# Squares added by VectorE, three last products by Pool, and gate blocks placed between a part's gates and its down products

## The chip, the cores and the metric

One core of one Trainium2 chip runs the kernel. The metric is the device time of one execution in microseconds (us), the median of several runs. The engines are named as the profile names them: PE (TensorE, with PEld for its weight loads), DVE (VectorE), ACT (ScalarE), POOL (GpSimd), and SP, whose queue issues all the DMAs here. Each engine executes its instructions in the order in which the program lists them; when the first waits, all behind it wait too.

## The reference, cut to what matters

The input x has 512 tokens of 1024 features. A block of four stages (a SwiGLU feed-forward, a mixer with a convolution and a recurrent scan, a second feed-forward, a norm) is followed by two layers, an "even" one (Fourier mixing and attention) and an "odd" one (a gated linear recurrence), and a last norm. The parts that this change touches:

```python
def rms_norm(x, g):
    xf = x.astype(jnp.float32)
    y = xf * lax.rsqrt(jnp.mean(xf * xf, axis=-1, keepdims=True) + RMS_EPS)
    return (y * g.astype(jnp.float32)).astype(x.dtype)

def swiglu(x, w_gate, w_up, w_down):      # 1024 -> 2816 -> 1024
    return (jax.nn.silu(x @ w_gate) * (x @ w_up)) @ w_down
...
    x = x + 0.5 * swiglu(rms_norm(x, ffn1_norm[l]), ...)
    x = x + token_mixer(rms_norm(x, mix_norm[l]), ...)
    x = x + 0.5 * swiglu(rms_norm(x, ffn2_norm[l]), ...)
    return rms_norm(x, final_norm)
```

The even layer begins with a second norm right behind `final_norm`, so two sums of squares of the same x are needed there: `s1` of x, and `s2` of x times the gain of `final_norm`.

## The kernel before

Features lie on the partitions: x is eight tiles `x[0]` to `x[7]` of 128 features by 512 tokens. Every product in float32 precision is made of three matmuls (`mm3`): each operand is split into a high part (`xh`, `h`, `wh`) and a low part (`xl`, `l`, `wl`), and high by high, low by high and high by low are added in one PSUM tile (`pm`). A `gemm` over 1024 features is thus 24 matmuls of 128x512.

A weight group (128x1024, 512 KB) takes this way: a DMA into `raw` (3 buffers), a cast to `wh` by ACT or DVE (4 buffers), a subtraction on DVE to `wl` (4 buffers). While the feed-forwards run, `put_low` also prepares the weights of later stages: it loads a group, splits it and stores its low part in DRAM (the DMA `low<-wl`), two groups for each of the gates 0 to 19 and one for each down product of the first two parts. The stage that needs them loads `raw` and `wl<-low`.

`rms` splits the scaled x, and `sumsq` squares the tiles on ACT and adds them up in `acc`, tile by tile, on Pool; `fold` splits `acc` into `h` and `l` and sums it over the partitions by two matmuls against ones (`rones`). In `ffn` 22 gates of 128 hidden features each are worked in three parts (8, 8 and 6). Gate `gi` is 24 matmuls for `pg`, 24 for `pu`; then DVE multiplies both by `rstd`, ACT takes the Silu, Pool multiplies the two, and ACT and DVE split the result into `h` and `l`. After the gates of a part come its eight down products (`ffn_d`), each a gemm over the part's `h` and `l`: three matmuls for each gate, the youngest gate's last. `last_norm` does the final norm in two halves of 256 tokens (`hf` 0 and 1); its last step multiplies the eight tiles by gain and by the reciprocal root (a PSUM tile) on DVE, and each product is stored by a DMA `y<-x`.

Nothing is issued as it is written. The kernel records its operations, and a list scheduler (`Rec.schedule`) simulates the engines offline with the costs of `_cost` and takes, on each engine, the ready operation of the lowest priority (its place in the written order plus a `bias`, for instance `late` for the sums of squares). The order found is then the order on the chip. All instructions therefore carry line L555 (`emit`).

Of the kernel before, what the change touches and what calls it, by code (L numbers as in the profile page):

```python
# [8 lines left out]
F32 = mybir.dt.float32  # L9
F32R = mybir.dt.float32r  # L10
AF = mybir.ActivationFunctionType
ALU = mybir.AluOpType
# [18 lines left out]
KT = 8  # L31
# [566 lines left out]
def _cost(o, outs, ins):  # L598

    n = _elems(outs[0]) if outs else 1  # L600
    psum = any("PSUM" in str(a.space) for a in ins)
    o.port = not any("PSUM" in str(a.space) for a in ins + outs) and n > 32 and o.fn not in ("tensor_reduce", "reciprocal")
    if o.eng == "tensor":
        if o.fn == "matmul":
            m = _elems(ins[0])
            k = int(ins[0].shape[0])
            up = lambda i: 32 if i <= 32 else 64 if i <= 64 else 128
            o.mode = up(k), up(m)
            one = "float32r" in str(ins[0].dtype)
            c = n / 2.4 + 13.5 if one else max(n, m) / 0.6 + 10.0  # L610
            o.load = n / (2.4 if one else 0.6) * o.mode[0] * o.mode[1] / 16384.0
            if not one and m <= 64 and k <= 64:
                c = 31.0 if n <= 64 else 105.0
        else:
            o.mode = 128, 128
            c = 109.0
            o.load = 50.0
        return c, 0.0
    if o.fn == "dma_start":
        run = min(_run(a) for a in outs + ins)  # L620
        return 480.0, _elems(outs[0]) * 4 * int(outs[0].shape[0]) / (360.0 if run >= 512 else 150.0)
    if o.eng == "scalar":
        c = 0.833 * n + (52.0 if psum else 94.0) + (185.0 if "accum_out" in o.kw else 0.0)
        return c + (93.0 if any(hasattr(o.kw.get(k), "tensor") for k in ("scale", "bias")) else 0.0), 0.0
    if o.eng == "gpsimd":
        k = {"memset": 0.76, "tensor_scalar": 1.2}.get(o.fn, 1.95)
        return k * n + 73.0, 0.0
    c = 69.0 if n > 16 else 105.0
    if o.fn == "tensor_tensor" and any(len(a.ap) > 1 and abs(list(a.ap)[-1][0]) >= 16 and list(a.ap)[-1][1] > 1 for a in ins):
        c += 0.9 * n  # L630
    if o.fn in ("tensor_scalar", "scalar_tensor_tensor"):
        c += 59.0 * sum(1 for a in ins[1:] if _elems(a) == 1 and n > 1)
    if o.fn == "reciprocal":
        return 6.25 * n + c, 0.0
    if o.fn == "tensor_tensor_scan":
        return 2.08 * n + c, 0.0
    if o.fn == "tensor_reduce":
        return 1.04 * _elems(ins[0]) + c, 0.0
    if o.fn in ("tensor_copy", "tensor_scalar", "memset") and not psum:
        return 0.52 * n + c, 0.0  # L640
    return 1.04 * n + c, 0.0
# [6 lines left out]
class Net:  # L648
    def __init__(self, tc, a, ctx, wbufs=(3, 4, 4), slots=76):
        self.tc, self.a = tc, a  # L650
        self.nc = self.rec = Rec(tc.nc)
        self.cp = ctx.enter_context(tc.tile_pool(name="cst", bufs=1))
        self.wp = ctx.enter_context(tc.tile_pool(name="wgt", bufs=1))
        self.wbufs = dict(zip(("raw", "wh", "wl"), wbufs))
        self.tp = ctx.enter_context(tc.tile_pool(name="act", bufs=1))
        self.sp = ctx.enter_context(tc.tile_pool(name="small", bufs=4))
        self.pm = ctx.enter_context(tc.tile_pool(name="pmm", bufs=8, space=PSUM))
        self.dp = ctx.enter_context(tc.tile_pool(name="dram", bufs=1, space=bass.MemoryType.DRAM))
        self.n = 0
        self.slots = slots  # L660
        self.late = 60
        self.low, self.later, self.behind, self.far = {}, [], 40, None
        nc = self.nc
        self.cst = self.cp.tile([128, _NC], F32, name="cst")
        self.vec = self.cp.tile([128, _NV], F32, name="vec")
        nc.sync.dma_start(out=self.vec, in_=a["vec"])
        self.load_x(a["xT"])
        nc.sync.dma_start(out=self.cst, in_=a["cst"])
        self.ident = self.c("ident")
        self.cr = {}  # L670
        for m in ("ones", "bones"):
            self.cr[m] = self.cp.tile([128, 128], F32R, name="r" + m)
            nc.vector.tensor_copy(self.cr[m], self.c(m))
        self.eps6 = self.cst[:, _COFF["eps"]:_COFF["eps"] + 1]
        self.epsg = self.cst[:, _COFF["eps"] + 1:_COFF["eps"] + 2]
        self.one = self.cst[:, _COFF["eps"] + 3:_COFF["eps"] + 4]
# [127 lines left out]
        self.nc.vector.scalar_tensor_tensor(l, src, g, h.bitcast(F32), op0=ALU.mult, op1=ALU.subtract)  # L804
        return h, l

    def sumsq(self, gains=None):

        nc = self.nc
        acc = self.T(p="acc")  # L810
        for k in range(KT):
            if k == 0:
                q = acc
            else:
                q = self.T(p="sq")
            if gains is None:
                nc.scalar.activation(q, self.x[k], AF.Square)
            else:
                nc.scalar.activation(q, self.x[k], AF.Square, scale=gains(k))
            if k:  # L820
                nc.gpsimd.tensor_tensor(acc, acc, q, ALU.add)
        ps = self.P()
        self.fold(ps, "ones", acc)
        return ps
# [16 lines left out]
        nc.vector.tensor_scalar(r, r, -0.5 * scale, 1.5, op0=ALU.mult, op1=ALU.add)  # L841
        nc.vector.tensor_tensor(out, out, r, ALU.mult)

    def rms(self, gname):

        xs = [self.split_scaled(self.x[k], self.v(gname, k)) for k in range(KT)]
        self.rec.bias = self.late
        ps = self.sumsq()
        rstd = self.T(p="rstd")
        self.rsqrt(rstd, ps, 1.0 / D, 1e-6)  # L850
        self.rec.bias = 0
        return xs, rstd


    def ffn(self, n):
        nc = self.nc
        xs, rstd = self.rms(n + "_norm")
        g0 = 0
        for ch, nk in enumerate((8, 8, 6)):
            hs = []  # L860
            for gi in range(g0, g0 + nk):
                wg = self.group(n + "_g", gi)
                pg = self.P()
                self.gemm(pg, wg, xs)
                wu = self.group(n + "_u", gi)
                pu = self.P()
                self.gemm(pu, wu, xs)
                t = self.T()
                nc.vector.tensor_tensor(t, pg, rstd, ALU.mult)
                nc.scalar.activation(t, t, AF.Silu)  # L870
                u = self.T()
                nc.vector.tensor_tensor(u, pu, rstd, ALU.mult)
                nc.gpsimd.tensor_tensor(u, u, t, ALU.mult)
                hs.append(self.split(u))
                if gi < 20:
                    self.put_low(2)
            g0 += nk
            for m in range(8):
                wd = self.group(f"{n}_d{ch}", m)
                ps = self.P()  # L880
                self.gemm(ps, wd, hs)
                xm = self.x[m]
                nc.vector.scalar_tensor_tensor(xm, ps, 0.5, xm, op0=ALU.mult, op1=ALU.add)
                if ch < 2:
                    self.put_low(1)


    def mixer(self):
# [457 lines left out]
    def _even(self):  # L1346
        nc = self.nc
        V, G, A, PE = nc.vector, nc.gpsimd, nc.scalar, nc.tensor
        x = self.x
# [1 line left out]
        o1, o2 = _VOFF["final_norm"], _VOFF["even_norm_2"]  # L1351
        V.tensor_tensor(g12, self.vec[:, o1:o1 + 8], self.vec[:, o2:o2 + 8], ALU.mult)
        xs = [self.split_scaled(x[k], g12[:, k:k + 1]) for k in range(KT)]
        s1 = self.sumsq()
        rstd1 = self.T(p="rs1")
        self.rsqrt(rstd1, s1, 1.0 / D, 1e-6)
        s2 = self.sumsq(lambda k: self.v("final_norm", k))
# [379 lines left out]
    def last_norm(self, hf):  # L1737
# [4 lines left out]
        s0 = slice(256 * hf, 256 * hf + 256)  # L1742
        if hf == 0:

            w = self.sm(1, tag="fw", bufs=1)
            o = A.activation(w, self.one, AF.Sqrt)
            o.deps.append(next(p for p in reversed(self.rec.ops[:-1]) if p.table))
        acc, q7 = (self.T(shape=(128, 512), p="sq")[:, 0:256] for _ in range(2))
        for k in range(KT):
            q = acc if k == 0 else q7 if k == KT - 1 else self.T(p="sq")[:, 0:256]  # L1750
            A.activation(q, x[k][:, s0], AF.Square)
            if 0 < k < KT - 1:
                G.tensor_tensor(acc, acc, q, ALU.add)
        on = self.c("ones")
        m = self.sm(2, tag="fn", bufs=8)
        for q, first in ((acc, True), (q7, False)):
# [16 lines left out]
        for t in range(2):  # L1773
            PE.matmul(ps[:, t * 128:t * 128 + 128], r[:, t:t + 1].to_broadcast([128, 128]), self.ident,
                      start=True, stop=True)
        for k in range(KT):
            V.scalar_tensor_tensor(x[k][:, s0], x[k][:, s0], self.v("final_norm_2", k), ps, op0=ALU.mult, op1=ALU.mult)
            nc.sync.dma_start(out=self.a["y"][:, k, s0], in_=x[k][:, s0])

    def all(self):  # L1780
# [2 lines left out]
        mix = [("w_in", t) for t in (5, 9, 1, 6, 10, 2, 7, 11, 3, 13, 17, 21, 14, 18, 22, 15, 19, 23, *range(26, 42))]  # L1783
        mix += [("w_out_a", h) for h in range(4)] + [("w_out_b", h) for h in range(4)] + [("w_o", g) for g in range(8)]
        n = len(self.rec.ops)
        self.later = mix
        self.ffn("ffn1")

        w = [o for o in self.rec.ops[n:] if o.fn == "dma_start"][:2]
        l = [o for o in self.rec.ops[:n] if o.fn == "dma_start"]  # L1790
# [31 lines left out]
```

## Time and profile before

| | |
|---|---|
| time, median of 3 runs | 1879.77 us (1878.92 to 1880.1) |
| the profiled execution's own time | 1883.26 us |
| its span from first to last instruction | 1881.5 us |
| mean granted clock of PE | 0.993 |
| busy share of PE, DVE, ACT, POOL | 98%, 68%, 45%, 13% |

The span leaves 1.76 us of the execution's time outside. A granted clock of 1.00 is full speed (2.4 GHz) and 0.5 half speed (1.2 GHz); a window in which part of the time was at half speed shows a number between.

### The profile page before, as it was taken

The page shows a single profiled execution, that of the slowest core. Times are in us where ns is not written, and L with a number is a line of the kernel's source. Part 1 is how long each engine was busy: PE and PEld are TensorE (multiplying, and loading weights), DVE is VectorE, ACT ScalarE, POOL GpSimd, SP SyncE. Part 2 cuts the span into 40 slices and gives each one's busy share as a digit, 9 for nine tenths or more (in the row PEclk, how much of TensorE's full clock was granted, in tenths as well). Part 3 has the DMA queues.
Part 4 walks back from the last instruction along what each step waited for, and adds up shares of the span by engine and source line. Part 5 has one row for each costly group of instructions (what it writes and reads, how often), then busy time and mean ns, then how long its engine had stood idle before and what let it go on. Part 6 is the DMA issues. An engine that isn't in the chain of part 4 may idle for free.

```text
span 1881.5 us, 26365 instructions
## 1 busy us (share of the span) xinstructions
PE 1842.7 (98%) x10324; PEld 1540.2 (82%) x10324; DVE 1272.1 (68%) x1956; ACT 852.2 (45%) x1180; POOL 246.4 (13%) x193
## 2 busy tenths in 40 slices
PE   7999999999999999999998999999999999999998
PEld 6878878887788887888887887888999888888887
DVE  7766665579857434477467567965478965899773
ACT  5333433365324333444344335422255554998771
POOL 2101100113203002211010017010000010000001
PEclk9999999999999999999999999999999999999999
DMA  7788896445533444578788773322221125556552
GB/s 249 271 302 282 293 299 201 121 152 162 179 121 112 152 137 160 197 260 308 251 281 288 252 261 107 115 66 69 90 68 59 65 79 191 178 191 211 191 179 102
DMA packets 120398, 341.10 MB, mean 181 GB/s; under 512 B 33872, under 2 KB 36176, under 8 KB 120272
## 3 DMA queue, kind: packets, MB, share of 16 engines
q1 hardware_dynamic: 120272, 339.41, 54.0%
q8 instruction: 81, 1.33, 0.3%
q14 instruction: 45, 0.37, 0.1%
HBM read 277.76 MB, written 61.60 MB: 180 GB/s over the span
## 4 chain that ended last, share of the span: by engine, by line
PE 73%; DMA 11%; DVE 11%; ACT 3%; issue 2%; POOL 0%; SPq 0%; DVEq 0%; ACTq 0%; POOLq 0%
PE pm L555 69%; DVE wl L555 5%; PE pw L555 4%; DMA low<-wl 2%; DMA raw<-o_in 2%; ACT wh L555 2%; DVE t L555 2%; DMA raw<-ffn_d 1%; DMA raw<-ffn_u 1%; DVE l L555 1%; DMA raw<-gw 1%; DMA raw<-w_in 1%; DMA raw<-w_out_a 1%; DVE wh L555 0%; DVE u L555 0%
## 5 line engine op out<-in xcount | busy, mean ns | idle before, releaser
L555 ACT CAST wh<-raw 128x1024 fp32r<-128x1024 f32 (+1 forms) x334 | 347.1, 1041 | 687.6 <-PE pm L555 278.4
L555 PE MATMUL pm<-xh,wh 128*128 128x512 f32 x1488 | 583.1, 392 | 8.4 <-ACT xh L555 8.2
L555 PE MATMUL pm<-xl,wh 128*128 128x512 f32 x1488 | 582.0, 391 | 2.5 <-DVE xl L555 2.5
L555 PE MATMUL pm<-xh,wl 128*128 128x512 f32 x1488 | 582.3, 391 | 1.1 <-DVE wl L555 1.0
L555 DVE TENSOR_TENSOR wl<-raw,wh 128x1024 fp32r<-128x1024 f32 (+1 forms) x302 | 386.3, 1282 | 202.2 <-DMA low<-wl 92.0
L555 PEld LDWEIGHTS pm<-xh,wh 128*128 128x128 f32 x1488 | 280.3, 188 | 67.2 <-ACT xh L555 9.4
L555 PEld LDWEIGHTS pm<-xl,wh 128*128 128x128 f32 x1488 | 280.4, 188 | 62.5 <-DVE xl L555 5.2
L555 PEld LDWEIGHTS pm<-xh,wl 128*128 128x128 f32 x1488 | 280.2, 188 | 60.5 <-DVE wl L555 2.8
L555 PE MATMUL pm<-h,wh 128*128 128x512 f32 (+1 forms) x832 | 319.1, 386 | 9.6 <-ACT h L555 9.0
L555 PE MATMUL pm<-l,wh 128*128 128x512 f32 (+1 forms) x832 | 319.9, 385 | 1.1 <-DVE l L555 1.1
L555 PE MATMUL pm<-h,wl 128*128 128x512 f32 (+1 forms) x832 | 319.5, 385 | 1.4 <-DMA wl<-low 1.2
L555 POOL TENSOR_TENSOR t<-t,t 128x512 f32<-128x512 f32 x60 | 88.8, 1481 | 932.1 <-DVE t L555 712.5
L555 PEld LDWEIGHTS pm<-h,wh 128*128 128x128 f32 x832 | 157.4, 190 | 42.8 <-ACT h L555 10.5
L555 PEld LDWEIGHTS pm<-l,wh 128*128 128x128 f32 x832 | 157.9, 190 | 33.7 <-DVE l L555 3.5
L555 PEld LDWEIGHTS pm<-h,wl 128*128 128x128 f32 x832 | 157.8, 190 | 32.1 <-DMA wl<-low 1.6
L555 DVE TENSOR_TENSOR t<-pm,rstd 128x512 f32<-128x512 f32 x146 | 98.8, 685 | 22.1 <-PE pm L555 17.6
L555 ACT ACT_TABLE_LOAD x71 | 91.1, 1283 | 24.8 <-DVE s L555 15.7
L555 DVE CAST wh<-raw 128x1024 fp32r<-128x1024 f32 x74 | 53.9, 728 | 58.2 <-PE pm L555 31.1
L555 POOL TENSOR_TENSOR acc<-acc,sq 128x512 f32<-128x512 f32 x42 | 66.2, 1584 | 140.0 <-ACT sq L555 139.7
L555 DVE TENSOR_TENSOR x<-x,pm 128x512 f32<-128x512 f32 (+1 forms) x44 | 27.9, 637 | 72.5 <-PE pm L555 70.4
L555 ACT ACTIVATE t<-t 128x512 f32<-128x512 f32 x100 | 59.7, 626 | 21.7 <-DVE t L555 20.1
L555 DVE TENSOR_TENSOR l<-t,h 128x512 fp32r<-128x512 f32 x87 | 61.0, 709 | 6.9 <-ACT h L555 5.5
(251 smaller groups left out, 2040.1 us busy)
## 6 DMA issues: line engine op xcount, KB each, us to landing
low<-wl SPq DMA_DIRECT2D x106, 512.0 KB, 3.8
wl<-low SPq DMA_DIRECT2D x106, 512.0 KB, 3.5
raw<-w_in SPq DMA_DIRECT2D x76, 512.0 KB, 4.7
raw<-o_in SPq DMA_DIRECT2D x64, 512.0 KB, 4.5
raw<-ffn_g SPq DMA_DIRECT2D x44, 512.0 KB, 4.4
raw<-ffn_u SPq DMA_DIRECT2D x44, 512.0 KB, 5.1
raw<-ffn_d SPq DMA_DIRECT2D x32, 512.0 KB, 5.1
raw<-o_out SPq DMA_DIRECT2D x32, 512.0 KB, 4.5
```

Source lines behind the costliest of these rows:

```text
L555: o.ins = getattr(getattr(self.nc, o.eng), o.fn)(*o.args, **o.kw)
```

## The change

Five things are altered. A tile `z` of zeros is set by Pool at the very start, ACT takes one square root of it (which loads ACT's table for roots), and PE makes 20 matmuls of `z` by `z` whose result nobody reads. The seven adds of the squares in the first feed-forward's norm and the seven of the even layer's first sum `s1` are made by DVE, no longer by Pool; the priority bias `late` is 100 in the first feed-forward. In both feed-forwards gate 8 is computed before the down products of the first part, gate 16 before those of the second part, and the last two down products of the second part stand behind gate 21. In the second half of the last norm ACT copies the reciprocal root from PSUM to `rs` and multiplies three tiles by the gain (`xg`), and Pool makes the products of these three. The planner's cost of an element on Pool goes from 1.95 to 2.4 ns, which moves instructions all through the program.

```diff
-    k = {"memset": 0.76, "tensor_scalar": 1.2}.get(o.fn, 1.95)
+    k = {"memset": 0.76, "tensor_scalar": 1.2}.get(o.fn, 2.4)
...
+        z = self.T(F32R, p="z")
+        nc.gpsimd.memset(z.bitcast(F32), 0.0)
+        nc.scalar.activation(self.sm(1, tag="fw", bufs=1), z[:, 0:1].bitcast(F32), AF.Sqrt)
+        ps = self.P()
+        for _ in range(20):
+            nc.tensor.matmul(ps, z[:, 0:128], z, start=True, stop=True)
...
-    def sumsq(self, gains=None):
+    def sumsq(self, gains=None, adds="gpsimd"):
...
-                nc.gpsimd.tensor_tensor(acc, acc, q, ALU.add)
+                getattr(nc, adds).tensor_tensor(acc, acc, q, ALU.add)
...
-        xs, rstd = self.rms(n + "_norm")
+        xs, rstd = self.rms(n + "_norm", "vector" if n == "ffn1" else "gpsimd")
+        hs = [[], [], []]
+
+        def gate(gi):
...
+            hs[gi // 8].append(self.split(u))
+            if gi < 20:
+                self.put_low(2)
+
+        def down(ch, m):
...
+        for gi in range(22):
+            gate(gi)
+            if gi in (8, 16):
+                for m in range(8 if gi == 8 else 6):
+                    down(gi // 8 - 1, m)
+        for m in (6, 7):
+            down(1, m)
+        for m in range(8):
+            down(2, m)
...
-        s1 = self.sumsq()
+        s1 = self.sumsq(adds="vector")
...
+        ng = 3 if hf else 0
+        xg = [self.T(shape=(128, 512), p="xg")[:, 0:256] for _ in range(ng)]
+        for k in range(ng):
+            A.activation(xg[k], x[k][:, s0], AF.Copy, scale=self.v("final_norm_2", k))
...
-        for k in range(KT):
-            V.scalar_tensor_tensor(x[k][:, s0], x[k][:, s0], self.v("final_norm_2", k), ps, op0=ALU.mult, op1=ALU.mult)
+        if hf:
+            rs = self.T(shape=(128, 512), p="rs")[:, 0:256]
+            A.copy(rs, ps)
+        for k in (*range(ng, KT), *range(ng)):
+            if k < ng:
+                G.tensor_tensor(x[k][:, s0], xg[k], rs, ALU.mult)
+            else:
+                V.scalar_tensor_tensor(x[k][:, s0], x[k][:, s0], self.v("final_norm_2", k), ps, op0=ALU.mult, op1=ALU.mult)
...
+        late, self.late = self.late, 100
```

**PE, second boundary of the second feed-forward.** Before: `pm_1812` is the second product of gate 15, `pm_1828` the first down product; `h_1675` is the split result of gate 8 and `h_1815` that of gate 15.

```order
L555 MATMUL pm_1812<-xl_1427,wh_1810 128x512
L555 MATMUL pm_1812<-xh_1426,wl_1811 128x512
L555 MATMUL pm_1828<-h_1675,wh_1826 128x512
L555 MATMUL pm_1828<-l_1676,wh_1826 128x512
...
L555 MATMUL pm_1828<-h_1795,wl_1827 128x512
L555 MATMUL pm_1828<-h_1815,wh_1826 128x512
L555 MATMUL pm_1828<-l_1816,wh_1826 128x512
```

After the change, the same place: `pm_1815` is the second product of gate 15, `pm_1831` and `pm_1835` the two of gate 16, `pm_1851` the first down product, and `h_1818` the result of gate 15.

```order
L555 MATMUL pm_1815<-xh_1429,wl_1814 128x512
L555 MATMUL pm_1831<-xh_1415,wh_1829 128x512
...
L555 MATMUL pm_1835<-xh_1429,wl_1834 128x512
L555 MATMUL pm_1851<-h_1614,wh_1849 128x512
L555 MATMUL pm_1851<-l_1615,wh_1849 128x512
...
L555 MATMUL pm_1851<-h_1818,wh_1849 128x512
```

Between the last matmul of gate 15 and the first that reads its result there stood 21 matmuls; now there stand 69, the 48 of gate 16 and the same 21.

**DVE, the start of the program.** Before: `xl_97` and `xl_99` are the low parts of `x[6]` and `x[7]`, `wl_135` and `wl_139` belong to gate 1, `wl_127` is a group prepared for later.

```order
L555 SCALAR_TENSOR_TENSOR xl_97<-x_80,vec,xh_96 128x512
L555 CAST rones<-cst 128x128
L555 CAST rbones<-cst 128x128
L555 SCALAR_TENSOR_TENSOR xl_99<-x_81,vec,xh_98 128x512
L555 TENSOR_TENSOR wl_135<-raw_133,wh_134 128x1024
L555 TENSOR_TENSOR wl_139<-raw_137,wh_138 128x1024
L555 TENSOR_TENSOR wl_127<-raw_125,wh_126 128x1024
```

After the change, the same place: `xl_100` and `xl_102` are the low parts of `x[6]` and `x[7]`, `wl_138` and `wl_142` belong to gate 1, `acc_103` is the sum of squares.

```order
L555 SCALAR_TENSOR_TENSOR xl_100<-x_83,vec,xh_99 128x512
L555 SCALAR_TENSOR_TENSOR xl_102<-x_84,vec,xh_101 128x512
L555 CAST rones<-cst 128x128
L555 CAST rbones<-cst 128x128
L555 TENSOR_TENSOR acc_103<-acc_103,sq_105 128x512
L555 TENSOR_TENSOR acc_103<-acc_103,sq_106 128x512
L555 TENSOR_TENSOR acc_103<-acc_103,sq_107 128x512
L555 TENSOR_TENSOR acc_103<-acc_103,sq_108 128x512
L555 TENSOR_TENSOR wl_138<-raw_136,wh_137 128x1024
L555 TENSOR_TENSOR acc_103<-acc_103,sq_109 128x512
L555 TENSOR_TENSOR wl_142<-raw_140,wh_141 128x1024
```

The low part of `x[7]` moved ahead of the two casts, and five of the seven adds stand ahead of the second subtraction of gate 1.

**DVE, the sums of the even layer.** After the change: `x_1382` is `x[7]`, `acc_2045` is `s1`, `acc_2058` is `s2` (still added on Pool), `l_2126` and `l_2128` are low parts of the Fourier tables.

```order
L555 SCALAR_TENSOR_TENSOR x_1382<-pm_2027,x_1382 128x512
L555 COPY t_2093<-raw_2091 1x512
L555 TENSOR_TENSOR wl_2103<-raw_2101,wh_2102 128x1024
L555 SCALAR_TENSOR_TENSOR xl_2044<-x_1382,g_2028,xh_2043 128x512
L555 TENSOR_TENSOR acc_2045<-acc_2045,sq_2052 128x512
L555 TENSOR_TENSOR l_2126<-t_2089,h_2125 128x512
L555 TENSOR_TENSOR l_2128<-t_2090,h_2127 128x512
L555 TENSOR_TENSOR l_2055<-acc_2045,h_2054 128x512
L555 TENSOR_TENSOR l_2068<-acc_2058,h_2067 128x512
```

Before, the same place reads, with `x_1379` as `x[7]`:

```order
L555 SCALAR_TENSOR_TENSOR x_1379<-pm_2024,x_1379 128x512
L555 COPY t_2089<-raw_2088 1x512
L555 TENSOR_TENSOR wl_2100<-raw_2098,wh_2099 128x1024
L555 SCALAR_TENSOR_TENSOR xl_2041<-x_1379,g_2025,xh_2040 128x512
L555 TENSOR_TENSOR l_2125<-t_2087,h_2124 128x512
L555 TENSOR_TENSOR l_2052<-acc_2042,h_2051 128x512
L555 TENSOR_TENSOR l_2065<-acc_2055,h_2064 128x512
```

The last add of `s1` moved from Pool into DVE's row behind the low part of `x[7]`, and one more low part stands ahead of the two that the folds need.

## Rows read from the trace of the kernel before

**Rows 1.** The page, part 4: the chain that ended last, by line.

```profile
PE pm L555 69%; DVE wl L555 5%; PE pw L555 4%; DMA low<-wl 2%; DMA raw<-o_in 2%; ACT wh L555 2%; DVE t L555 2%; DMA raw<-ffn_d 1%; DMA raw<-ffn_u 1%; DVE l L555 1%; DMA raw<-gw 1%; DMA raw<-w_in 1%; DMA raw<-w_out_a 1%; DVE wh L555 0%; DVE u L555 0%
```

**Rows 2.** Windows: stretch, length, busy (count) of PE, PEld, DVE, ACT, POOL; PE clock, DMA share, GB/s.

```profile
0.00:30.00 30.00, 20.13 (x71) 14.60 (x72) 20.82 (x18) 15.91 (x23) 11.24 (x11) 1.00 0.67 234
30.00:100.00 70.00, 70.00 (x309) 57.69 (x308) 57.18 (x57) 29.35 (x35) 11.38 (x7) 1.00 0.77 270
100.00:120.00 20.00, 17.23 (x61) 12.99 (x60) 13.03 (x16) 6.39 (x7) 1.28 (x1) 0.83 0.93 320
240.00:250.00 10.00, 8.60 (x37) 6.57 (x36) 6.21 (x9) 4.65 (x5) 1.76 (x2) 1.00 0.84 279
1010.00:1030.00 20.00, 14.14 (x49) 10.78 (x49) 13.55 (x16) 8.38 (x9) 1.26 (x1) 0.83 0.87 297
1160.00:1180.00 20.00, 16.02 (x56) 11.77 (x55) 16.81 (x17) 11.80 (x17) 15.15 (x8) 0.83 0.41 121
1600.00:1700.00 100.00, 100.00 (x443) 82.81 (x442) 89.77 (x135) 90.75 (x136) 0.00 (x0) 1.00 0.54 188
```

**Rows 3.** Waits of PE over the span: in total, how often, the longest.

```profile
PE pm L555 <- ACT h L555: 13.4, 5, 5.9
PE pm L555 <- DVE wl L555: 1.3, 2, 1.0
```

**Rows 4.** Timeline of the start, PE: start, length, instruction, idle before and its releaser.

```profile
8.23 0.79 PE L555 MATMUL pm<-xh,wh 128*128 128x512 f32 x1 [8.23 <-ACT xh L555]
10.47 0.63 PE L555 MATMUL pm<-xl,wh 128*128 128x512 f32 x1
10.90 0.63 PE L555 MATMUL pm<-xh,wl 128*128 128x512 f32 x1
...
20.83 0.50 PE L555 MATMUL pm<-xl,wh 128*128 128x512 f32 x1 [1.17 <-DVE xl L555]
```

**Rows 5.** Timeline of the start, ACT, DVE and POOL.

```profile
6.17 1.28 ACT L555 ACT_TABLE_LOAD   x1 [6.17 <-DMA x<-xT]
...
20.70 5.67 DVE L555 TENSOR_TENSOR wl<-raw,wh 128x1024 fp32r<-128x1024 f32 x3
...
15.64 8.51 POOL L555 TENSOR_TENSOR acc<-acc,sq 128x512 f32<-128x512 f32 x5 [0.84 <-ACT sq L555]
```

**Rows 6.** Timeline, first feed-forward, first boundary: weights on DVE, and PE.

```profile
101.25 1.23 DVE L555 TENSOR_TENSOR wl<-raw,wh 128x1024 fp32r<-128x1024 f32 x1 [1.24 <-DMA low<-wl]
...
102.53 0.50 PE L555 MATMUL pm<-h,wl 128*128 128x512 f32 x1 [0.23 <-DVE wl L555]
...
109.09 0.73 PE L555 MATMUL pm<-h,wh 128*128 128x512 f32 x2 [1.92 <-ACT h L555]
```

**Rows 7.** Groups of instructions of DVE and ACT: busy us, mean ns of one.

```profile
L555 DVE TENSOR_TENSOR t<-t,t 128x512 f32<-128x512 f32 x54 | 34.8, 682 | 5.4 <-ACT t L555 5.2
L555 ACT COPY R<-pw 128x256 f32<-128x256 f32 x32 | 10.6, 389 | 15.7 <-PE pw L555 15.7
```

**Rows 8.** Timeline, second feed-forward, second boundary: DVE and PE.

```profile
1017.61 1.23 DVE L555 TENSOR_TENSOR wl<-raw,wh 128x1024 fp32r<-128x1024 f32 x1 [1.85 <-DMA low<-wl]
1018.76 0.68 DVE L555 TENSOR_TENSOR t<-pm,rstd 128x512 f32<-128x512 f32 x1
...
1021.97 0.79 PE L555 MATMUL pm<-h,wh 128*128 128x512 f32 x1 [5.86 <-ACT h L555]
```

**Rows 9.** Timeline of the even layer's sums: DVE, POOL, PE.

```profile
1164.28 1.78 DVE L555 SCALAR_TENSOR_TENSOR xl<-x,g,xh 128x512 fp32r<-128x512 f32 x1
1168.55 0.73 DVE L555 SCALAR_TENSOR_TENSOR xl<-x,g,xh 128x512 fp32r<-128x512 f32 x1
...
1165.47 7.98 POOL L555 TENSOR_TENSOR acc<-acc,sq 128x512 f32<-128x512 f32 x4
...
1172.94 0.79 PE L555 MATMUL pm<-h,rones 128*128 128x512 f32 x1 [2.87 <-ACT h L555]
```

**Rows 10.** Timeline of the end: SP's issues of the last eight stores.

```profile
1875.30 3.77 SPq L555 DMA_DIRECT2D y<-x  x8
```

More of the change, by code (lines that the diff above doesn't have):

```diff
@@ L842, in rsqrt, with rms @@
         nc.vector.tensor_tensor(out, out, r, ALU.mult)
-    def rms(self, gname):
+    def rms(self, gname, adds="gpsimd"):
         xs = [self.split_scaled(self.x[k], self.v(gname, k)) for k in range(KT)]
         self.rec.bias = self.late
-        ps = self.sumsq()
+        ps = self.sumsq(adds=adds)
         rstd = self.T(p="rstd")
@@ L856, in ffn @@
         nc = self.nc
-        xs, rstd = self.rms(n + "_norm")
[L858 to L885, printed above, removed]
+        xs, rstd = self.rms(n + "_norm", "vector" if n == "ffn1" else "gpsimd")
@@ new lines, in ffn @@
+        hs = [[], [], []]
+        def gate(gi):
+            wg = self.group(n + "_g", gi)
+            pg = self.P()
+            self.gemm(pg, wg, xs)
+            wu = self.group(n + "_u", gi)
+            pu = self.P()
+            self.gemm(pu, wu, xs)
+            t = self.T()
+            nc.vector.tensor_tensor(t, pg, rstd, ALU.mult)
+            nc.scalar.activation(t, t, AF.Silu)
+            u = self.T()
+            nc.vector.tensor_tensor(u, pu, rstd, ALU.mult)
+            nc.gpsimd.tensor_tensor(u, u, t, ALU.mult)
+            hs[gi // 8].append(self.split(u))
+            if gi < 20:
+                self.put_low(2)
@@ new lines, in down @@
+        def down(ch, m):
+            wd = self.group(f"{n}_d{ch}", m)
+            ps = self.P()
+            self.gemm(ps, wd, hs[ch])
+            xm = self.x[m]
+            nc.vector.scalar_tensor_tensor(xm, ps, 0.5, xm, op0=ALU.mult, op1=ALU.add)
+            if ch < 2:
+                self.put_low(1)
+        for gi in range(22):
[5 more added lines that the diff above has]
+            down(1, m)
@@ L1743, in last_norm @@
         if hf == 0:
-            w = self.sm(1, tag="fw", bufs=1)
+            w = self.sm(1, tag="fx", bufs=1)
             o = A.activation(w, self.one, AF.Sqrt)
@@ L1785, in all @@
         n = len(self.rec.ops)
+        late, self.late = self.late, 100
         self.later = mix
         self.ffn("ffn1")
+        self.late = late
         w = [o for o in self.rec.ops[n:] if o.fn == "dma_start"][:2]
```

## The prediction

> **What bounds the kernel now.** I read the chain that ended last first: two thirds of it are PE's matmuls into `pm`, and the largest entries besides are the weights on their way (DVE `wl` 5%, the store `low<-wl` 2%) [rows 1]. So PE is the bound, and time can only come from places where PE is not at its full pitch. The windows give them. The stretch 1600 to 1700 holds 443 matmuls of 128x512 in 100 us, 0.2257 us each; 30 to 100 holds 309 in 70, the same pitch. What a window lost is its length less its matmuls times 0.2257. By that 0 to 30 lost 30 − 71 × 0.2257 = 14.0 us, 100 to 120 lost 6.2, 240 to 250 lost 1.65, 1010 to 1030 lost 8.9 and 1160 to 1180 lost 7.4 [rows 2]. These five are the places of the change: the start, the boundaries between gates and down products, and the sums of the even layer. Together they are 38 us, 2% of the span. The waits of PE say who is waited for: the high part `h`, 13.4 us in five waits, while weights (`wl`) cost only 1.3 [rows 3]. The windows with a mean granted clock of 0.83 show that a loss is more than its wait: after the wait the matmuls run for some microseconds at half clock. In 1010 to 1030 the wait is 5.86 of the 8.9.
>
> **The start.** The first real matmul is at 8.23; the next ones follow at 10.47, 10.90, a pitch of 0.43, twice the usual: half clock. At 20.83 PE waits 1.17 for the low part of `x[7]` [rows 4]. ACT loads its table at 6.17 when `x[0]` is there, 1.28 us before it can scale. Five adds on Pool hold from 15.64 to 24.15, and three subtractions on DVE beside them take 5.67, 1.89 each [rows 5], where one without Pool takes 1.23 [rows 6]. The change moves the table load ahead, takes Pool out, puts the low part of `x[7]` ahead of two casts, and lets PE run 20 dummies. These are 20 × 0.43 = 8.6 us at the half pitch, somewhat less if the clock rises under them; they start once Pool has set `z`, so they end at 8 to 10 and the first real matmul stays at about 8.3. What they can give is the pitch: the first twelve matmuls take from 8.23 to about 14.1 now, 2.7 at full pitch, so 3.1 at most. Then gate 0 has to wait for the data all the same. Next is the weight of gate 1: its `wl` begins at 20.70 now, and in the new row it stands behind four adds of 0.68 [rows 7] and two casts. With subtractions of 1.23 instead of 1.89, I place it at 21.0 at its end where it ends at 22.6 now, while PE asks for it first at 25.3 now. PE gains at most the 4.2 between 21.0 and 25.3; the third gate's loads, which wait for the second subtraction of gate 1 (25.2 now, some 22.9 then), gain 2.3. I take −3, bounds 0 (PE waits for the weights anyway) and −5.
>
> **The boundaries.** The first down product needs the youngest gate's `h` at its 22nd matmul. In the first feed-forward PE stands at 109.09 after 1.92 us for it, and the clock falls [rows 6]. In the second the DVE row shows why: the multiplication of the second product waits behind a subtraction that itself waited 1.85 us for the store `low<-wl`, and PE stands 5.86 us [rows 8]. After the change a whole gate lies between: 48 × 0.2257 = 10.8 us more cover. The longest wait of PE for `h` is 5.9 [rows 3], so the waits end; and with them the half clock behind. At the third boundary two down products, 10.8 us as well, give the same cover. At most it gives 6.2 + 1.65 + 8.9 = 16.8 us. But the wait also let the weights get ahead: at 102.48 a `wl` is finished and at 102.53 PE uses it, having waited 0.23 [rows 6]. A gate asks for g, u and two groups for later with their two stores, 6 × 0.5 MB in 10.8 us or 290 GB/s; that stretch ran at 270 before the boundary and 320 in it, with DMA at 0.93 [rows 2]. The DMAs can deliver about what PE asks for without the pause, not much more. What is queued behind a late weight is everything on PE. I keep about four fifths: −4.5 (bounds −2 and −6.2) at the first, −1.4 (0 and −1.65) at the second, −7.5 (−4 and −8.9) in the second feed-forward.
>
> **The even layer's sums.** PE waits 2.87 us for `h` of `s1` until 1172.94, since Pool is adding for both sums: four adds from 1165.47 take 7.98, 2.0 each [rows 9], where an add on DVE takes 0.68 [rows 7]. Seven adds more on DVE are 4.8 us of work beside PE; DVE is 16.8 of 20 us busy there [rows 2], and only the last add matters, behind `xl` of `x[7]`. I place `h` at about 1170.8, two microseconds earlier. The low part `l` then stands behind two other low parts of 0.7, and the second sum stays on Pool, so PE keeps a bit under 2 us of short waits. Whether the clock falls again is open: 1.92 us and half clock went together at 109.09, and 240 to 250 lost 1.65 with its clock at 1.00. I take −3.5, halfway; bounds 0 and −6.
>
> By the Trainium skill ("SBUF — State Buffer", Who interferes with whom) a DVE instruction with two SBUF inputs and a GpSimd instruction that reads SBUF exclude each other for a whole instruction. The trace bears out that they slow each other: `xl` beside Pool takes 1.78 against 0.73 [rows 9]. What it would make of the sum is the second rival.
>
> **The end.** Pool takes three of eight products, but the stores are issued by SP one in 0.47 us, 3.77 for eight [rows 10]; the issue sets the end, not the products. In front of them ACT now copies the root from PSUM, 0.39 by the nearest row [rows 7], and the first product on DVE waits for that; behind it stand four products and all eight stores. So +0.45, bounds 0 and +0.6.
>
> **The rest.** The new cost of Pool reorders instructions everywhere; at full pitch PE hides it (1600 to 1700). I take 0, bounds −2 and +2.
>
> **The sum.** −3 − 4.5 − 1.4 − 7.5 − 3.5 + 0.45 = −19.45 us. The profiled execution had 1881.5 of span and 1.76 around it, 1883.26; that gives 1863.8. It was 3.5 us above the median of the runs shown, so in their terms 1879.77 − 19.45 = 1860.3; I say 1860.5.
>
> **The rivals.** *The weights take it back.* PE that no longer pauses finds its weights late, as at 102.53, and half of the gain at the start and the boundaries (16.4 / 2 = 8.2) becomes waits for `wl`: about 1868.5. For it speaks the lead of 0.05 us; against it the total wait for weights, 1.3 us, and the 320 GB/s that the DMAs reached. *The even layer's stall stays.* If each of DVE's adds is held up by Pool like `xl`, some 1.05 more, then the last `xl` and the last add end about 2.1 later, `h` comes at 1172.9 as now, and the gain there is nothing: about 1864. *The start gives nothing*, since the dummies end late (10) and the clock falls before the data come: about 1864, or with 1.5 lost 1865. *Slower.* One mechanism could do it: weights late by more than 1.9 us, in gate after gate, with the clock halved each time. The boundary at 100 to 120 prices such an event at 6.2 us. It takes three to cancel the gain and four or more to be slower, say five for 1891; nothing in the 70 us from 30 to 100, where the lead was smallest, lost any pitch, so this is unlikely.
>
> **How the numbers follow.** Forecast 0.53 (its own range 1856 to 1864.5); weights 0.22; even stall 0.11; start 0.07; slower 0.03; and 0.04 for the weights taking nearly all. 0.2% is 3.8 us, about what a measurement of this kernel can tell from no change. Faster is all but the last two, 0.93; same 0.04; slower 0.03. With every term but the rest at its far bound the sum would be −27.75, 1852; the range reaches from 1854 to 1870, which takes in the first three rivals.
>
> **What would show it.** Right: the first `pm<-h` of each down part without a wait on `h`; clock 1.00 in the windows around both former boundaries; in the even layer a first fold before 1171 on the old scale; the first dozen real matmuls at 0.23; the store of `y` begun 0.4 later behind the last matmul and still eight issues of 0.47. Wrong: waits of PE for `wl` well over 1.3 us in all, in gates 8 and 16 above all, and windows with a clock below 1 where there was none.

## The result and the profile after

| | before | after |
|---|---|---|
| time, median | 1879.35 us (1877.19 to 1880.1, 4 runs) | 1858.03 us (1856.3 to 1861.21, 4 runs) |
| ratio | | 0.9893, 95% interval 0.9877 to 0.9909 |
| profiled execution, its span | 1883.26, 1881.5 | 1858.05, 1856.3 |

The change makes the kernel 20 us faster by the ratio (17 to 23), 21.3 by the medians. 1860.5 was forecast, with a range of 1854 to 1870.

The windows of the changed kernel, with the columns of [rows 2]: the start, the first and second boundary of the first feed-forward (now near 108 and 239), the second boundary of the second feed-forward (near 1010), and the even layer's sums.

```profile
0.00:30.00 30.00, 28.26 (x113) 22.38 (x114) 21.09 (x27) 18.28 (x27) 0.73 (x5) 1.00 0.80 279
95.00:125.00 30.00, 30.00 (x134) 24.83 (x133) 21.30 (x23) 10.73 (x12) 2.58 (x2) 1.00 0.89 307
235.00:255.00 20.00, 20.00 (x90) 16.57 (x89) 12.59 (x16) 8.31 (x9) 1.76 (x2) 1.00 0.88 296
995.00:1035.00 40.00, 40.00 (x178) 33.12 (x177) 28.30 (x32) 15.87 (x17) 3.86 (x3) 1.00 0.91 313
1135.00:1165.00 30.00, 26.83 (x115) 20.96 (x114) 25.99 (x30) 18.97 (x27) 14.45 (x5) 1.00 0.45 143
```

At the three boundaries PE is busy to the last tenth and the clock is 1.00; [rows 2] had 0.83 at two of them. In the first 30 us, 93 of the 113 matmuls are real (20 are dummies) against 71 before: the loss there falls from 14.0 to 30 − 93 × 0.2257 = 9.0 us. The even layer still loses 30 − 115 × 0.2257 = 4.0.

Four of PE's waits over the span, to set beside [rows 3]:

```profile
PE pm L555 <- ACT h L555: 2.2, 1, 2.2
PE pm L555 <- DMA wl<-low: 2.1, 1, 2.1
PE pm L555 <- POOL z L555: 1.3, 1, 1.3
PE pm L555 <- DVE wl L555: 1.1, 2, 0.9
```

The wait for `h` is 2.2 in one place instead of 13.4 in five, and that one place is in the even layer. The wait for `wl<-low`, a low part loaded from DRAM, is in the mixer; it was 1.2 before, and behind it the clock fell in this trace, where the first trace of before kept 1.00 (as `after_again` did too):

```profile
725.00:745.00 20.00, 17.39 (x68) 13.83 (x69) 14.63 (x18) 8.56 (x12) 12.24 (x8) 0.91 0.82 299
```

That is one of the signs of being wrong that the prediction named, if a small one. The timeline of the start, which answers to [rows 4] and [rows 5], PE and DVE:

```profile
1.31 6.76 PE L555 MATMUL pm<-z 128*128 128x512 f32 x20 [1.31 <-POOL z L555]
7.91 0.39 PE L555 MATMUL pm<-xh,wh 128*128 128x512 f32 x1
8.13 0.39 PE L555 MATMUL pm<-xl,wh 128*128 128x512 f32 x1
...
10.84 4.06 DVE L555 SCALAR_TENSOR_TENSOR xl<-x,vec,xh 128x512 fp32r<-128x512 f32 x6
15.08 3.08 DVE L555 TENSOR_TENSOR acc<-acc,sq 128x512 f32<-128x512 f32 x4
18.08 1.22 DVE L555 TENSOR_TENSOR wl<-raw,wh 128x1024 fp32r<-128x1024 f32 x1
```

The real matmuls begin at 7.91 at a pitch of 0.22, all low parts of x are done by 14.9 (`x[7]` at 20.8 before), and the subtraction of gate 1 ends at 19.3; I had placed it at 21.0.

**Where the time went, stage by stage.** Counting the matmuls of the traces along PE's order of issue gives the moments at which PE first uses the low part of certain weights: gate 2 of the first feed-forward, the mixer's first group, gate 0 of the second feed-forward, the first and the fourth Fourier group of the even layer. The lengths between, in us, for all fourteen traces (the experiments are told below):

```
kernel         to gate 2  ffn1 rest  mixer   ffn2    even    rest    span
before             36.6      346.4   410.0   369.7    24.6   694.2  1881.5
before_again       36.2      342.7   409.8   364.5    23.7   694.5  1871.4
cost_only          35.7      337.7   407.9   367.4    23.9   693.7  1866.3
gates_only         37.0      338.8   409.5   360.2    24.8   693.8  1864.0
no_gates           32.1      341.4   408.7   368.2    21.4   694.9  1866.7
after              31.8      337.3   410.0   361.4    21.4   694.4  1856.3
after_again        32.4      337.3   407.7   360.8    21.4   694.5  1854.1
no_dummies         34.4      339.4   408.2   360.2    22.9   694.5  1859.6
start_pool         34.6      337.3   408.4   360.2    23.0   694.3  1857.7
even_pool          32.3      337.3   409.6   359.5    23.3   694.1  1856.0
even_both          31.9      338.5   410.9   362.6    19.0   694.5  1857.5
end_dve            32.0      338.3   408.9   360.2    23.0   694.0  1856.3
ring5              32.5      337.3   406.1   360.2    22.8   694.6  1853.5
short_form         32.1      337.3   409.7   359.5    22.1   694.2  1854.9
```

The mean of the two traces of before less the mean of the two of after is 4.3 at the start, 7.3 in the rest of the first feed-forward, 1.1 in the mixer, 6.0 in the second feed-forward, 2.8 in the even layer and about nothing in the rest: 21.3 in all. (In `even_both` a wait of 2.98 us for a weight falls just ahead of the border between the second feed-forward and the even layer.)

### The profile page after: what moved, and what is told of

It reads as the page before. It is cut to its first block, busy times and chain, and to the rows that moved or that the text cites. A ratio compares the mean times of both kernels' runs of the same rounds, so it can differ in the third digit from the quotient of the medians.

```text
span 1856.3 us, 26407 instructions
## 1 busy us (share of the span) xinstructions
PE 1835.8 (99%) x10344; PEld 1540.4 (83%) x10344; DVE 1266.8 (68%) x1966; ACT 854.5 (46%) x1188; POOL 230.5 (12%) x182
## 4 chain that ended last, share of the span: by engine, by line
PE 53%; DMA 6%; DVE 5%; ACT 1%; issue 1%; POOL 1%; SPq 0%; POOLq 0%; DVEq 0%; ACTq 0%
PE pm L555 51%; DMA raw<-o_in 3%; PE pw L555 2%; DVE wl L555 2%; DMA low<-wl 2%; ACT wh L555 1%; DMA raw<-ffn_d 1%; DVE t L555 0%; DVE l L555 0%; DMA wl<-low 0%; POOL acc L555 0%; DVE x L555 0%; DVE xl L555 0%; DVE acc L555 0%; DVE s L555 0%
## 5 line engine op out<-in xcount | busy, mean ns | idle before, releaser
L555 POOL TENSOR_TENSOR acc<-acc,sq 128x512 f32<-128x512 f32 x28 | 46.7, 1667 | 151.1 <-ACT sq L555 151.1
```

The source lines that it names most:

```text
L555: o.ins = getattr(getattr(self.nc, o.eng), o.fn)(*o.args, **o.kw)
```

## The experiments

**The gates alone, and all but the gates.** `gates_only` is the kernel before with only the new loops of `ffn` (the adds stay on Pool); `no_gates` is the changed kernel with the old loops.

```diff
 # gates_only, against before
-        for ch, nk in enumerate((8, 8, 6)):
...
+        for gi in range(22):
+            gate(gi)
+            if gi in (8, 16):
...
 # no_gates, against after: the reverse
```

> The kernel before with only the new order of gates and down products in both feed-forwards. Theory (the gates cover the wait for h, and the parts of the change add up): the three boundaries give what they gave in the trace of the changed kernel, 6.8 + 2.3 + 9.2 less 1.7 taken back by late weights, so 16 to 18 us less than before, about 1862. Rival (weights take it back): without the cushion of the pause the weights are late and half of it is lost, 8 to 9 us less, about 1871, with waits of PE for wl of 5 us or more.

Measured: 1865.74 us (1864.1 to 1866.92) beside 1877.96 of before, ratio 0.9934 (0.9921 to 0.9948), 12.2 us less by the medians. The gain is between the two forecasts, and PE waits 1.9 us for `wl` in all, not the 5 or more of the rival.

> The changed kernel with the old order of gates and down products. Theory: 16 to 18 us slower than the changed kernel, about 1875, with waits for h at the boundaries and a clock below 1.00 there. Rival (the parts are not additive: the faster start alone puts the weights ahead of PE or PE ahead of the weights): the difference is under 10 us or over 22.

Measured: 1868.51 us, ratio 0.9951 (0.9939 to 0.9964) to before, some 11 us slower than the changed kernel, not 16 to 18 and just outside the rival's under 10. So the parts don't add up. The windows of `no_gates` at the two boundaries that were the dearest before:

```profile
100.00:120.00 20.00, 18.49 (x81) 14.67 (x80) 13.67 (x15) 6.83 (x7) 1.30 (x1) 1.00 0.93 314
1000.00:1020.00 20.00, 17.51 (x69) 13.77 (x68) 13.12 (x16) 8.28 (x9) 1.29 (x1) 0.91 0.89 306
```

They lose 20 − 81 × 0.2257 = 1.7 and 20 − 69 × 0.2257 = 4.4 us. The old loops do stall, but for less than the 6.2 and 8.9 of [rows 2]. Two questions followed: whether the first trace was a dear one, and what else in the change shortens these boundaries.

**The kernel before, once more.** Nothing is edited.

> The kernel before once more, for a second trace. Theory (the profiled execution of before was one in which the second boundary of the second feed-forward was late by more than usual): the wait for h there is 2 to 4 us where the first trace had 5.86, the window 1010 to 1030 loses 3 to 6 us where it lost 8.9, and the span is near 1876. Rival (that wait is the same in every execution, and the new order of the gates gives less for another reason): 5 to 6 us again.

Measured: 1878.45 us (1873.3 to 1881.09, 10 runs), ratio 1.0002 (0.9992 to 1.0011). The profiled execution has a span of 1871.4, 10 us less than the first. Its windows at the first feed-forward's two boundaries and the second one of the second, and PE's wait in the last:

```profile
100.00:120.00 20.00, 17.45 (x69) 13.22 (x68) 14.20 (x15) 6.40 (x7) 1.28 (x1) 0.91 0.91 319
240.00:250.00 10.00, 10.00 (x45) 8.05 (x44) 7.79 (x11) 2.86 (x4) 0.00 (x0) 1.00 0.88 301
1005.00:1025.00 20.00, 17.32 (x75) 13.75 (x74) 13.81 (x15) 8.28 (x9) 1.28 (x1) 1.00 0.86 294
```

```profile
1014.45 0.50 PE L555 MATMUL pm<-h,wh 128*128 128x512 f32 x1 [2.45 <-ACT h L555]
```

The same program loses 4.4, nothing and 3.1 here where the first trace had 6.2, 1.65 and 8.9. The theory held (the span was expected near 1876): what the boundaries cost differs from one execution to the next, and the trace on which I worked was one of the dear ones. All times of before taken here reach from 1873.3 to 1883.43.

**The planner's new cost of Pool alone.**

```diff
 # cost_only, against before
-    k = {"memset": 0.76, "tensor_scalar": 1.2}.get(o.fn, 1.95)
+    k = {"memset": 0.76, "tensor_scalar": 1.2}.get(o.fn, 2.4)
```

> The kernel before with only the planner's new cost of Pool. Theory (it moves instructions under full cover): within 2 us of the kernel before. Rival (the new order is what shortens the boundaries and the even layer in the changed kernel): 3 us or more faster.

Measured: 1868.48 us beside 1879.84 of before, ratio 0.9948 (0.9935 to 0.9962), 11.4 us less by the medians and 9.8 by the ratio. My theory fell here. The windows of `cost_only` at the first boundary of the first feed-forward and the second one of the second, and PE's wait in the latter:

```profile
100.00:120.00 20.00, 20.00 (x90) 16.56 (x89) 14.47 (x16) 6.84 (x7) 1.29 (x1) 1.00 0.93 322
1000.00:1020.00 20.00, 14.88 (x58) 11.55 (x56) 13.77 (x15) 8.35 (x9) 1.26 (x1) 0.83 0.85 293
```

```profile
1009.54 0.80 PE L555 MATMUL pm<-h,wh 128*128 128x512 f32 x1 [5.12 <-ACT h L555]
```

In the first feed-forward the stall is gone without any gate in between (337.7 us in the table, as with the gates); in the second it is all there, 20 − 58 × 0.2257 = 6.9. The rows of DVE, Pool and ACT around the first boundary tell the difference. Before:

```profile
103.57 0.69 DVE L555 CAST wh<-raw 128x1024 fp32r<-128x1024 f32 x1 [0.50 <-DMA raw<-w_in]
104.30 1.23 DVE L555 TENSOR_TENSOR wl<-raw,wh 128x1024 fp32r<-128x1024 f32 x1
105.44 0.68 DVE L555 TENSOR_TENSOR t<-pm,rstd 128x512 f32<-128x512 f32 x1
...
106.27 1.28 POOL L555 TENSOR_TENSOR t<-t,t 128x512 f32<-128x512 f32 x1 [9.12 <-DVE t L555]
...
107.48 1.04 ACT L555 CAST wh<-raw 128x1024 fp32r<-128x1024 f32 x1 [0.23 <-DMA raw<-w_in]
108.43 0.61 ACT L555 CAST h<-t 128x512 fp32r<-128x512 f32 x1
```

With the new cost:

```profile
99.02 1.23 DVE L555 TENSOR_TENSOR wl<-raw,wh 128x1024 fp32r<-128x1024 f32 x1
100.73 0.69 DVE L555 TENSOR_TENSOR t<-pm,rstd 128x512 f32<-128x512 f32 x1 [0.49 <-PE pm L555]
...
102.15 1.05 ACT L555 CAST wh<-raw 128x1024 fp32r<-128x1024 f32 x1 [0.24 <-DMA raw<-w_in]
103.11 0.61 ACT L555 CAST h<-t 128x512 fp32r<-128x512 f32 x1
```

The order of these rows is the same in both. PE ends the second product of the part's last gate at 101.85 before and at 100.70 here. Before, DVE multiplies it by `rstd` only 3.6 us later, at 105.44, behind the cast and the subtraction of a weight for a later stage whose load came late, in a row that had also waited 1.24 us for the store `low<-wl` [rows 6]; here the multiplication follows PE at once. ACT adds the smaller part: before, Pool ends its product at 107.55, and the cast of `h` begins 0.9 later, behind a weight cast that waited for its load. The loads land about 5.3 us earlier with the new cost, while PE is only 1.1 us ahead. So `h` comes in time. The wait for `h` was a wait for weights: what stood in its way, on DVE above all, was work on weights whose load or store was late.

**The start: without the dummies, and with the adds on Pool.**

```diff
 # no_dummies, against after
-        ps = self.P()
-        for _ in range(20):
-            nc.tensor.matmul(ps, z[:, 0:128], z, start=True, stop=True)
 # start_pool, against after
-        xs, rstd = self.rms(n + "_norm", "vector" if n == "ffn1" else "gpsimd")
+        xs, rstd = self.rms(n + "_norm")
```

> The changed kernel without the 20 matmuls of zeros (the early table load stays). Theory (they give the clock): the first dozen real matmuls run at a pitch of 0.43, but begin about 1.1 us earlier, and the weights of gate 1 leave a slack of 1.2 us: 1 to 2 us slower than the changed kernel. Rival (the start's gain of 4.8 us is all clock): 4 us slower or more. Second rival (it is all DVE's and ACT's): no difference.

Measured: 1860.8 us, ratio 0.991 (0.9896 to 0.9925), against 0.9893 for the changed kernel: 3 us more by the ratios, with overlapping intervals. PE at the start of `no_dummies`:

```profile
7.15 0.79 PE L555 MATMUL pm<-xh,wh 128*128 128x512 f32 x1 [7.15 <-ACT xh L555]
...
8.96 0.63 PE L555 MATMUL pm<-xh,wh 128*128 128x512 f32 x1
9.38 0.63 PE L555 MATMUL pm<-xl,wh 128*128 128x512 f32 x1
...
27.41 0.39 PE L555 MATMUL pm<-h,rones 128*128 128x512 f32 x1
```

The first real matmul is 0.8 earlier, but at half clock; the fold of the squares, a fixed place in PE's order, is at 27.41 where the changed kernel has it at 24.76. So the dummies are worth 2.7 us there, more than the 1 to 2 expected.

> The changed kernel with the adds of the first feed-forward's norm back on Pool; the low part of the last tile then stands behind the two casts again. Theory (the start's gain is mostly DVE's: subtractions of 1.2 instead of 1.9 us and the low part in time): 2 to 3.5 us slower than the changed kernel, with a wait for xl of about 1 us near 20 and subtractions beside Pool of 1.8 or more. Rival (it is the dummies and the table): no difference, since without the dummies 2 to 3 us were lost.

Measured: 1860.08 us, ratio 0.9908 (0.9893 to 0.9923), again some 3 us more than the changed kernel. PE and DVE of `start_pool`:

```profile
20.17 0.50 PE L555 MATMUL pm<-xl,wh 128*128 128x512 f32 x1 [1.17 <-DVE xl L555]
...
20.03 5.67 DVE L555 TENSOR_TENSOR wl<-raw,wh 128x1024 fp32r<-128x1024 f32 x3
```

The wait for `xl` and the subtractions of 1.89 are back, as [rows 4] and [rows 5] had them. Neither forecast held alone. Both halves of the start's gain are needed: with the clock alone PE waits for DVE, and with DVE alone PE is slow. To gate 2 it takes 34.4 and 34.6 us without one of them, between 36.4 before and 32.1 with both, so each is worth somewhat over 2. The early table load is in all of these; its own share was not measured.

**The even layer: the first sum back on Pool, and both sums on DVE.**

```diff
 # even_pool, against after
-        s1 = self.sumsq(adds="vector")
+        s1 = self.sumsq()
 # even_both, against after
-        s2 = self.sumsq(lambda k: self.v("final_norm", k))
+        s2 = self.sumsq(lambda k: self.v("final_norm", k), adds="vector")
```

> The changed kernel with the adds of the even layer's first sum back on Pool. Theory: 3.2 us slower than the changed kernel (the gain seen there between the first and the third group of the Fourier weights), with a wait of about 2.9 us for h and half clock behind it. Rival (the second sum on Pool is what PE waits for in both): under 1 us.

Measured: 1857.1 us, ratio 0.9888 (0.9874 to 0.9901): no slower than the changed kernel.

> The changed kernel with the adds of both sums of the even layer on DVE. Theory (in the changed kernel PE waits 2.2 us at the fold for the second sum, which is still on Pool): that wait goes, 1 to 2 us faster than the changed kernel. Rival (DVE has no room there, 20 of 20 us busy ahead of the folds): the low parts of x come later, PE waits for xl in place of h, no difference or up to 2 us slower.

Measured: 1857.34 us, ratio 0.9891 (0.9877 to 0.9906): no difference either. The traces say why. In the changed kernel, PE, ACT and POOL at the sums:

```profile
1150.41 0.50 PE L555 MATMUL pm<-h,rones 128*128 128x512 f32 x1 [2.19 <-ACT h L555]
...
1146.81 0.62 ACT L555 CAST h<-acc 128x512 fp32r<-128x512 f32 x1 [0.19 <-DVE acc L555]
1149.74 0.62 ACT L555 CAST h<-acc 128x512 fp32r<-128x512 f32 x1 [2.31 <-POOL acc L555]
...
1142.82 1.28 POOL L555 TENSOR_TENSOR acc<-acc,sq 128x512 f32<-128x512 f32 x1
1144.33 5.38 POOL L555 TENSOR_TENSOR acc<-acc,sq 128x512 f32<-128x512 f32 x1 [0.23 <-ACT sq L555]
```

`h` of the first sum is ready at 1147.43, but the last add of the second sum, alone on Pool now, takes 5.38 us where the one ahead of it took 1.28: it runs while DVE issues one two-input instruction behind the other. The last of them is

```profile
1147.91 0.67 DVE L555 TENSOR_TENSOR l<-acc,h 128x512 fp32r<-128x512 f32 x1
```

and Pool ends at 1149.71, 1.13 us behind it, not much less than an add alone takes. PE waits for that instead. With the first sum on Pool PE waits for `xl`, and with both on DVE for a weight, each the only wait of over 1 us there; `even_pool` first, then `even_both`:

```profile
1146.19 0.80 PE L555 MATMUL pm<-xl,wh 128*128 128x512 f32 x1 [2.80 <-DVE xl L555]
```

```profile
1144.06 0.50 PE L555 MATMUL pm<-xh,wl 128*128 128x512 f32 x1 [2.98 <-DVE wl L555]
```

Which of three products is late depends on who does the adds. That DVE and Pool together bound this stretch fits these rows; no run took work off both, so it is not shown.

**The end: all products on DVE.** `end_dve` has the changed kernel's `last_norm` without `xg` and `rs`, as before.

> The changed kernel with all eight last products on DVE, straight from PSUM, and the stores in the old order. Theory (the issue of the stores sets the end): 0.2 to 0.5 us faster than the changed kernel, which is too little to tell from it by time; in the trace the first store is issued 0.3 to 0.5 earlier behind the last matmul, and eight issues take 3.8 again. Rival (the products set the end): 1 us or more slower.

Measured: 1857.63 us, ratio 0.9892 (0.9875 to 0.9908), the same as the changed kernel. Products and stores, of the changed kernel first, whose PE ends its last matmuls at 1848.77:

```profile
1849.21 2.05 DVE L555 SCALAR_TENSOR_TENSOR x<-x,vec,pm 128x256 f32<-128x256 f32 x5 [1.27 <-ACT rs L555]
1849.26 2.10 POOL L555 TENSOR_TENSOR x<-xg,rs 128x256 f32<-128x256 f32 x3 [5.40 <-ACT rs L555]
1849.72 3.77 SPq L555 DMA_DIRECT2D y<-x  x8
```

And of `end_dve`, whose PE ends them at 1848.63 + 0.68 = 1849.31:

```profile
1849.35 3.22 DVE L555 SCALAR_TENSOR_TENSOR x<-x,vec,pm 128x256 f32<-128x256 f32 x8 [0.87 <-PE pm L555]
1849.86 3.77 SPq L555 DMA_DIRECT2D y<-x  x8
```

The products take 2.15 us from the first's begin to the last's end with Pool's help instead of 3.22, and the eight issues still take 3.77; they begin 0.95 after the last matmul with the copy, 0.55 without. That is +0.40 where +0.45 was forecast, and nothing gained.

**The changed kernel again, with a fifth buffer, and without what gave nothing.** These ran side by side.

```diff
 # ring5, against after
-    def __init__(self, tc, a, ctx, wbufs=(3, 4, 4), slots=76):
+    def __init__(self, tc, a, ctx, wbufs=(3, 4, 5), slots=74):
 # short_form, against after (last_norm as before, too)
-        for _ in range(20):
+        for _ in range(16):
...
-        s1 = self.sumsq(adds="vector")
+        s1 = self.sumsq()
```

> The changed kernel once more, for a second trace and as the measure of the runs beside it. Theory (the old boundaries scattered by execution, the new ones don't): 1856 to 1860, no wait for h at the feed-forwards' boundaries, clock 1.00 there; the waits for wl in the gates 9 to 11 of the second feed-forward may be there or not. Rival: waits for h return at the boundaries in some executions, 5 us or more above the first trace.

Measured: 1859.14 us (1855.84 to 1861.2), ratio 0.9895 (0.9877 to 0.9912), span 1854.1 in its trace, no wait for `h` at the feed-forwards' boundaries. The theory held; the waits for `wl` in the second feed-forward came again.

> The changed kernel with five buffers for wl in place of four (and two fewer tiles for activations). Theory (the weights are late in the second feed-forward since DVE's subtractions wait for a buffer that the store low<-wl still reads): DVE's wait for low<-wl falls from 87 us to under 60, leads grow by a microsecond or more, and the time falls by 1 to 2 us. Rival (the loads themselves are late): no difference in time, leads in the second feed-forward still under 1 us at the least.

Measured: 1855.43 us (1854.01 to 1855.68), ratio 0.9875 (0.9856 to 0.9894), 3.7 less than `after_again` beside it, all of whose runs lie above; the two intervals of the ratios overlap. DVE's wait for the store, in the changed kernel and in `ring5`:

```profile
DVE wl L555 <- DMA low<-wl: 86.7, 59, 4.6
```

```profile
DVE wl L555 <- DMA low<-wl: 13.5, 18, 1.7
```

The least lead of a weight over PE in the second feed-forward (the time from its subtraction's end to PE's first use) rises from 0.05 to 7.9 us: with the buffer the weights are no longer late. How much time that gives is less clear. The stage takes 360.2 us where the changed kernel had 361.4 and 360.8, but `gates_only`, `no_dummies`, `start_pool` and `end_dve` have 360.2 with four buffers, so late weights cost something in some executions only; the largest gain in this trace is in the mixer, 406.1 against 410.0 and 407.7. By its time this version beats both kernels.

> The changed kernel without the parts that gave nothing: all last products on DVE, the even layer's first sum on Pool, and 16 dummies in place of 20, since the dummies end 1.3 us after the first xh is there. Theory: 0.5 to 2 us faster than the changed kernel, and the first real matmul near 6.9. Rival (16 are too few for the clock): the first real matmuls at a pitch of 0.43 and 1 to 3 us slower.

Measured: 1857.31 us (1855.95 to 1858.06), ratio 0.9886 (0.987 to 0.9902): at most 2 us better than `after_again`, within the runs' spread. PE starts on real work at 7.39, at full pitch, but then waits for `xl` twice, 0.2 each, so the half microsecond is given back.

## Why the prediction was right

The change does what was said at the start and at the boundaries, and the sum (−19.45 against −20 by the ratio) is right, in part by luck, as the terms below show. By terms, against the mean of two traces of each kernel:

- **The start** gave 4.3 (forecast 3, bounds 0 to 5). The mechanism is as described, clock and DVE both. The size was off because DVE's work ahead of the four adds ended earlier than I placed it (all low parts at 14.9), so gate 1's weight was there at 19.3, not 21.0, although the adds took 0.77 each, not 0.68.
- **The boundaries of the first feed-forward** gave 7.3 (forecast 5.9), those of the second 6.0 in the whole stage (forecast 7.5). The waits for `h` ended and the clock stayed up. The bounds from one trace (6.2, 1.65 and 8.9) were those of one execution; the second trace has 4.4, 0 and 3.1. Measured from the mean of both, these places had 12.1 to give, not 16.8.
- **The weights take it back**, the first rival, in part: the changed kernel waits 0.89 for a weight in the second feed-forward, behind a DVE row that waited for the store `low<-wl`:

```profile
931.65 1.23 DVE L555 TENSOR_TENSOR wl<-raw,wh 128x1024 fp32r<-128x1024 f32 x1 [4.01 <-DMA low<-wl]
...
932.93 0.50 PE L555 MATMUL pm<-xh,wl 128*128 128x512 f32 x1 [0.89 <-DVE wl L555]
```

  From gate 9 to gate 15 that stage lost 1.7 us in one trace of the changed kernel and 1.0 in the other, not 8. I kept four fifths of 16.8 for it, 13.4, and the two stages gave 13.3; that this is so near is luck, since the 16.8 was too much and the stages also gained elsewhere. I had looked for the cause in the DMAs' rate; in `ring5`, with a fifth buffer, the late weights are gone.
- **The even layer** gave 2.8 in the traces (forecast 3.5), but undoing it costs nothing: `even_pool` is as fast. And 2.8 is not firm: in the trace of `end_dve`, which differs from the changed kernel only at the end, the stage took 23.0, not 21.4: behind the same wait the clock fell there. The step "the second sum stays on Pool, so PE keeps a bit under 2 us of short waits" was right in kind (2.19 in one wait, and 0.91 for `xl`), and by the time this term is nil within what can be told.
- **The SBUF rival.** By the Trainium skill ("SBUF — State Buffer", Who interferes with whom) a DVE instruction with two SBUF inputs and a GpSimd one that reads SBUF exclude each other. The trace agrees that they hurt each other, with 5.38 us for an add of 1.28, but it was Pool that lost here, to six DVE instructions in a row, not DVE as in my rival: DVE's `xl` took 0.73.
- **The end** cost 0.40, as forecast.
- **The rest** failed. "The new cost of Pool reorders instructions everywhere; at full pitch PE hides it (1600 to 1700). I take 0, bounds −2 and +2" is wrong: the cost alone gives about 10 us (7 to 12 by its interval). At the first boundary of the first feed-forward loads and casts come earlier with it, and PE's stall there was late weights at bottom. The sum came out right because the gates cover the same stall. In the table, against the mean of before, the rest of the first feed-forward gains 6.9 with the cost alone, 5.8 with the gates alone and 7.3 with both; the second gains nothing with the cost alone and 6.9 with the gates. By the medians the two alone are 11.4 and 12.2; together with the start's 4.3 they should have made 28, and the whole is 21.

What stays open is which of the moves that the new cost makes brings the loads forward; no run took them apart. Nor did one give the kernel before a fifth buffer with the old loops, which might end the same stalls without the gates.

## What to carry to other kernels

A wait names the last thing that came, not the cause: follow the chain back one engine at a time to where a row first falls behind, and if a cast or subtraction there waits for a load or a store, count the buffers it waits for before reordering the work. Where two edits mend the same stall, price them apart as well as together; their gains don't add. And take a second trace of the kernel before, since a stall that is a race with the DMAs has no one size.

## What the runs showed of the hardware

- A wait of PE does not price itself. At the second feed-forward's boundary 5.86 us of wait were followed by half clock [rows 2, 8], and so were 1.92 at the first boundary [rows 2, 6]; 2.45 us in `before_again` were not (its window has 1.00). Even one and the same wait does both. For the second sum of the even layer PE waits 2.19 us in the changed kernel, with a clock of 1.00 in the window shown above, and 2.19 us in `end_dve` (at 1149.30), with 0.94 in the same window:

```profile
1135.00:1165.00 30.00, 26.31 (x105) 20.32 (x105) 25.02 (x29) 17.32 (x25) 13.33 (x5) 0.94 0.42 140
```

  Of the seven traces with this wait (2.15 to 2.20), the clock stays up in `after`, `after_again` and `no_gates`, where the stage takes 21.4, and falls in `no_dummies`, `start_pool`, `end_dve` and `ring5`, where it takes 22.8 to 23.0. That prices the fall at 1.4 to 1.6 us.
- Matmuls of zeros whose result nobody reads left the clock up: behind them the first real ones ran at a pitch of 0.22 (7.91, 8.13), where they ran at 0.42 without (8.96, 9.38). The clock column can't show this: it has 1.00 for 0 to 30 in both kernels, though the kernel before began at a pitch of 0.43 [rows 2, 4].
- A Pool add of 1.28 us took 5.38 beside DVE at work, and ended 1.13 us after the last of six two-input DVE instructions in a row: as far as this shows, Pool got no turn between them. An exact rule for who yields can't be read from these rows: beside Pool, DVE's `xl` took 1.78 in one trace [rows 9] and 0.73 in another.
